# Two residual mixer layers in float32r: the operand's hi and lo parts side by side, one 512-column matmul for the hi weights

## The chip, the cores and the metric

The kernel runs on one core of one Trainium2 chip. The metric is the device time of one execution in microseconds (us). TensorE (PE) multiplies, VectorE (DVE) and ScalarE (ACT) do the elementwise work, GpSimd (POOL) does a little, SyncE (SP) issues most transfers. PEld is the weight load that goes ahead of each matmul.

## The reference

Two layers work on 256 tokens of 2048 channels. A vector c gives each layer six modulation vectors (shift, scale and gate, for the mixer and for the feed-forward):

```python
mod = cond @ w_ada[i] + b_ada[i]
h = rmsnorm(x, g_pre_mix[i]) * (1.0 + sc1) + sh1
z = h @ w_in[i]            # 2048 -> the inputs of two token mixers (GLA and RWKV-7)
...
y = jnp.concatenate([o_gla, o_rwkv], axis=-1) @ w_out[i]
x = x + gt1 * rmsnorm(y, g_post_mix[i])
h = rmsnorm(x, g_pre_ffn[i]) * (1.0 + sc2) + sh2
y = jnp.square(jax.nn.relu(h @ w_ff1[i])) @ w_ff2[i]     # 2048 -> 8192 -> 2048
x = x + gt2 * rmsnorm(y, g_post_ffn[i])
```

Everything is float32.

## The kernel before

Activations are kept channel-major: 128 channels on the partitions, 256 tokens in the free dimension, 16 such k-tiles. Each large product goes over weight tiles of 1 MB: 2048 inputs by 128 outputs. So that a fast float32r matmul keeps float32 accuracy, both sides are split into two parts. `split` (L295) rounds half of a weight tile (128x1024) to hi on ACT (L299), and takes lo = weight - hi on DVE (L300). The activations are split in the same way when they are made (hh and hl, or hid with two halves). `block_steps` (L303) then does, for each of 16 k-tiles, three matmuls of 256 columns into one half of a PSUM bank: hi weights by hi operand (L311), hi by lo (L312), lo by hi (L313). Each of them loads its own 128x128 weights. Below, one k-tile of one weight tile is called a triple.

`wtile` (L283) issues the load of a weight tile on SP's queue into one of three `wraw` buffers and splits it into four buffers of hi and four of lo, so that the split can be two weight tiles ahead. It does this at a priority that is put `AHEAD` = 100 instructions forward in the program; the scheduler of the framework orders each engine's instructions by priority when the kernel is built, and each engine then takes its queue in order. In between, `wtile` lets in modulation jobs (`ada_job`, L251): 1 MB of `w_ada` into a `wraw` buffer, and one DVE reduction of 128x2048 (L256).

The stages of a layer, in order:
- The mixers. Weight tiles of w_in are multiplied as `ORDER` says (k, q, h, g and v words), and between groups of four k-tiles (`QUANTUM`) the dependent chains of both mixers take a step: small plain float32 matmuls, ACT and DVE operations on 128x256 tiles out of a pool of 13 (`f256`). Blocks k and v leave PSUM through `lerp` (L486: ACT, then DVE); q and k of the GLA by one ACT operation each (L979, L981); gates g are read from PSUM by tanh and by DVE (L1008, L1010); the values h are a product the other way round (L993 to L995: weights are the tokens of hh and hl, moving are 256 columns of hi and lo) and leave by an ACT copy (L1000).
- w_out: 16 blocks of the mixed outputs (L1041), which leave by an ACT operation (L1042) and a square for the norm's sum.
- `boundary` (L376): residual, norm, and the first seven blocks of the next product, which grow k-tile by k-tile with `grow` (L348).
- The feed-forward, in four chunks of 16 hidden blocks: ff1 (L1061) with relu on ACT (L1068), square on DVE (L1070), split on ACT and DVE (L1072, L1073), at a priority 50 instructions ahead; then ff2 (L1077), 16 blocks that are added up over the chunks by one DVE operation a block (L1081; L1079 copies in the first chunk). Its blocks lie in six PSUM banks in turn.

The first layer's feed-forward spreads 64 modulation jobs over 118 weight tiles, the second's 16 over 100.

Of the kernel before, what the change touches and what calls it, by code (L numbers as in the profile page):

```python
# [20 lines left out]
KAPPA = 0.6065306597126334  # exp(-0.5)  # L21

# columns of the per-channel parameter table
# [65 lines left out]
GROW_LAG = 8  # pairs of k-tiles by which the first blocks' products lag behind their operand  # L89
# [7 lines left out]
def _finish(gen):  # L97
    """runs a generator to its end."""
    while True:
        try:  # L100
            next(gen)
        except StopIteration as e:
            return e.value


class Chains:
    """dependent work of several engines, in steps that are put in between the weight products."""
# [25 lines left out]
    def side_step(self):  # L133
        """one step of the chain with a pace of its own."""
# [12 lines left out]
    def run(self, blocks):  # L147
        """the blocks' steps, with the chains' steps in between."""
# [14 lines left out]
class Kernel:  # L163
    def __init__(self, tc, ctx, a):
# [4 lines left out]
        self.whi = pool("whi", 4)  # L169
        self.wlo = pool("wlo", 4)  # L170
# [9 lines left out]
    def setup(self, pool):  # L180
        nc, a, c = self.nc, self.a, self.const
        # c on four partitions
# [12 lines left out]
        # silu(c), then on all partitions  # L195
# [9 lines left out]
        # small numbers that guard roots, as bias columns  # L205
# [36 lines left out]
    def tanh(self, out, in_, bias=0.0, scale=1.0, more=()):  # L242
        """tanh, and back to the tables that the rest of the kernel uses."""
# [7 lines left out]
    def ada_job(self, i, j, single=None):  # L251
        """single: a pool for a job whose outputs are needed at once."""
# [11 lines left out]
    def ada_done(self, i, j0, j1):  # L264
        """bias, and the products with the norms' weights (and with what their roots leave out)."""
# [4 lines left out]
        # shift, scale, gate of the mixer, then of the feed-forward  # L270
# [24 lines left out]
    def split(self, half, w):  # L295
        n = half.shape[1]
        hi = self.whi.tile([P, D // 2], F32R, name="hi")[:, :n]
        lo = self.wlo.tile([P, D // 2], F32R, name="lo")[:, :n]
        self.nc.scalar.copy(hi, half)  # L299
        self.nc.vector.tensor_tensor(lo, half, hi.bitcast(F32), op=ALU.subtract)  # L300
        return hi.rearrange("p (k c) -> p k c", c=w), lo.rearrange("p (k c) -> p k c", c=w)

    def block_steps(self, src, xh, xl, order=range(KT), ps=None):  # L303
        """[128 outputs, tokens] = tile^T @ x over 16 k-tiles, in a PSUM tile."""
        nc = self.nc
        parts = self.wtile(src, P)
        if ps is None:
            ps = self.psm.tile([P, 512], F32, name="pm")[:, :T]
# [28 lines left out]
    def total(self, tiles):  # L337
        """sum over partitions (and over the tiles) on every partition."""
# [5 lines left out]
    def new_h(self):  # L344
        self.hh = self.hp.tile([P, KT, T], F32R, name="hh")
        self.hl = self.hp.tile([P, KT, T], F32R, name="hl")

    def grow(self, hi, lo, xh, xl, k, m0=0):  # L348
        """one k-tile more for the first blocks."""
# [7 lines left out]
    def first_norm(self, pool, rstd):  # L357
        """the first layer's h, k-tile by k-tile as its modulation comes in, and the first blocks of its product."""
# [6 lines left out]
        for k in range(KT):  # L365
# [8 lines left out]
            self.grow(hi, lo, self.hh[:, k], self.hl[:, k], k)  # L374
# [51 lines left out]
    def first_block(self, n, out):  # L426
        """a first block after its factor: on out, without its shift, and the shift."""
# [811 lines left out]
```

## Time and profile before

| | |
|---|---|
| median of 3 runs | 2784.63 us (2783.07 to 2787.88) |
| span of the profiled execution | 2786.0 us |
| PE / weight loads busy | 95% / 92% |
| DVE / ACT busy | 72% / 51% |
| HBM | 235 GB/s over the span |

The profile is one execution, taken by the hardware profiler. Its span runs from the first to the last instruction; the runs' times are those of executions without a profile. Matmuls are pipelined, so a record of one overlaps the next: the distance from start to start is what one costs in a stream, not its duration. "L311" is line 311 of the kernel. The names of operands are those of the program.

### The profile page before, as it was taken

The numbers are of one execution on the slowest core, as the hardware profiler recorded it, in microseconds if no ns is written. First come the engines' busy times: TensorE is split into PE (matmuls) and PEld (weight loads), VectorE is DVE, ScalarE is ACT, GpSimd is POOL, SyncE is SP. The second block draws the span as 40 slices with busy tenths as digits, with TensorE's granted clock in tenths as the row PEclk, the third lists the DMA queues.
The fourth block names the chain that finished last, engine by engine and source line by source line (L and its number), as shares of the span: only waits on it lengthen the run. The fifth ranks groups of instructions, "written<-read, shape, count | busy, mean of one in ns | idle before, by whom it ended". The sixth has DMA issues, their size and how long they took to land.

```text
span 2786.0 us, 55551 instructions
## 1 busy us (share of the span) xinstructions
PE 2658.6 (95%) x23388; PEld 2551.7 (92%) x23388; DVE 1997.1 (72%) x2961; ACT 1421.5 (51%) x2357; POOL 59.2 (2%) x153
## 2 busy tenths in 40 slices
PE   5689999999999999999999999999999999999997
PEld 4678888898999999999988889888989999999997
DVE  8997986678867777777777798655785465565655
ACT  3378644445644434434577875444474443443443
POOL 0000000000000000000001000000000000000000
PEclk8799999999999999999999999998999999999999
DMA  9775576576777777777745547654845666666653
GB/s 402 312 278 196 182 279 239 208 271 231 254 287 289 275 284 284 286 281 282 282 176 206 205 154 264 224 175 159 327 157 212 213 213 218 218 213 212 212 184 119
DMA packets 104082, 659.20 MB, mean 237 GB/s; under 512 B 11540, under 2 KB 20884, under 8 KB 32408
## 3 DMA queue, kind: packets, MB, share of 16 engines
q1 hardware_dynamic: 87848, 618.19, 61.5%
q10 hardware_dynamic: 15984, 37.46, 3.7%
q8 instruction: 183, 3.00, 0.4%
q14 instruction: 67, 0.55, 0.1%
HBM read 638.83 MB, written 16.78 MB: 235 GB/s over the span
## 4 chain that ended last, share of the span: by engine, by line
PE 84%; DVE 9%; DMA 3%; ACT 3%; issue 2%; ACTq 0%; POOL 0%; DVEq 0%; SPq 0%
PE pm L311 14%; PE pm L313 14%; PE pm L312 14%; PE px L312 8%; PE px L313 8%; PE px L311 8%; DVE raw L256 3%; DVE lo L300 2%; PE p L504 1%; DMA raw<-in_wout_dram 1%; PE pm L993 1%; PE pm L994 1%; PE px L451 1%; PE pm L995 1%; ACT hi L299 1%
## 5 line engine op out<-in xcount | busy, mean ns | idle before, releaser
L300 DVE TENSOR_TENSOR lo<-raw,hi 128x1024 fp32r<-128x1024 f32 (+1 forms) x792 | 959.7, 1216 | 544.3 <-ACT hi L299 537.8
L299 ACT CAST hi<-raw 128x1024 fp32r<-128x1024 f32 (+1 forms) x792 | 822.3, 1043 | 800.6 <-PE pm L312 356.1
L311 PE MATMUL pm<-hh,hi 128*128 128x256 f32 x2624 | 762.5, 291 | 3.6 <-ACT hi L299 1.5
L313 PE MATMUL pm<-hh,lo 128*128 128x256 f32 x2624 | 750.4, 286 | 3.9 <-DVE lo L300 3.9
L312 PE MATMUL pm<-hl,hi 128*128 128x256 f32 x2624 | 749.9, 286 | 0.0
L311 PEld LDWEIGHTS pm<-hh,hi 128*128 128x128 f32 x2624 | 504.5, 192 | 14.1 <-issue 2.0
L313 PEld LDWEIGHTS pm<-hh,lo 128*128 128x128 f32 x2624 | 504.9, 192 | 8.9 <-DVE lo L300 5.2
L312 PEld LDWEIGHTS pm<-hl,hi 128*128 128x128 f32 x2624 | 505.4, 193 | 4.6 <-issue 1.6
L256 DVE CUSTOM_DVE_ANT_0 raw<-raw,cond 128x2048 f32<-128x2048 f32 x192 | 439.0, 2287 | 38.3 <-DMA raw<-in_ada_dram 37.8
L313 PE MATMUL pm<-hid,lo 128*128 128x256 f32 x1024 | 289.0, 282 | 0.0
L313 PE MATMUL px<-hid,lo 128*128 128x256 f32 x1024 | 288.3, 282 | 0.0
L312 PE MATMUL px<-hid,hi 128*128 128x256 f32 x1024 | 288.2, 281 | 0.0
L312 PE MATMUL pm<-hid,hi 128*128 128x256 f32 x1024 | 288.0, 281 | 0.0
L311 PE MATMUL pm<-hid,hi 128*128 128x256 f32 x1024 | 287.2, 280 | 0.0
L311 PE MATMUL px<-hid,hi 128*128 128x256 f32 x1024 | 287.1, 280 | 0.0
L313 PE MATMUL px<-hh,lo 128*128 128x256 f32 x896 | 253.6, 283 | 0.0
L311 PE MATMUL px<-hh,hi 128*128 128x256 f32 x896 | 253.5, 283 | 0.0
L312 PE MATMUL px<-hl,hi 128*128 128x256 f32 x896 | 253.5, 283 | 0.0
L311 PEld LDWEIGHTS px<-hid,hi 128*128 128x128 f32 x1024 | 194.5, 190 | 0.0
L311 PEld LDWEIGHTS pm<-hid,hi 128*128 128x128 f32 x1024 | 194.4, 190 | 0.0
L313 PEld LDWEIGHTS pm<-hid,lo 128*128 128x128 f32 x1024 | 193.1, 189 | 0.0
L313 PEld LDWEIGHTS px<-hid,lo 128*128 128x128 f32 x1024 | 193.0, 189 | 0.0
(333 smaller groups left out, 4184.4 us busy)
## 6 DMA issues: line engine op xcount, KB each, us to landing
raw<-in_ff_dram SPq DMA_DIRECT2D x242, 1024.0 KB, 4.9
raw<-in_ada_dram SPq DMA_DIRECT2D x192, 1024.0 KB, 6.2
raw<-in_win_dram SPq DMA_DIRECT2D x90, 1024.0 KB, 5.1
raw<-in_wout_dram SPq DMA_DIRECT2D x32, 1024.0 KB, 5.4
raw<-in_ff1s_dram SPq DMA_DIRECT2D x16, 896.0 KB, 4.6
spill<-pk ACTq DMA_DIRECT2D x16, 640.0 KB, 4.1
pk<-spill ACTq DMA_DIRECT2D x16, 640.0 KB, 5.0
raw<-in_w_dram SPq DMA_DIRECT2D x16, 512.0 KB, 10.5
```

The costliest lines, as they stand in the source:

```text
L256: nc.vector.tensor_tensor_reduce(out=raw, in0=raw, in1=self.cond, op0=ALU.mult, op1=ALU.add, scale=1.0, scalar=0.0, accum_out=self.mod[:, ...
L299: self.nc.scalar.copy(hi, half)
L300: self.nc.vector.tensor_tensor(lo, half, hi.bitcast(F32), op=ALU.subtract)
L311: nc.tensor.matmul(ps, hi[:, n % 8], xh(k), start=n == 0, stop=False)
L312: nc.tensor.matmul(ps, hi[:, n % 8], xl(k), start=False, stop=False)
L313: nc.tensor.matmul(ps, lo[:, n % 8], xh(k), start=False, stop=n == KT - 1)
L451: self.nc.tensor.matmul(ps, self.ones, sq[:, q], start=k + q == 0, stop=k + q == KT - 1)
L504: self.nc.tensor.matmul(v[:, h, n + c], l[hs, cs], r[hs, cs], start=True, stop=True)
L993: nc.tensor.matmul(vps[c], hh[:, kk, cs], hi[:, kq], start=kk == 0, stop=False)
L994: nc.tensor.matmul(vps[c], hl[:, kk, cs], hi[:, kq], start=False, stop=False)
L995: nc.tensor.matmul(vps[c], hh[:, kk, cs], lo[:, kq], start=False, stop=kk == KT - 1)
```

## The change

The operand's hi and lo parts are put side by side in one tile ([128, 16, 2, 256]), and a PSUM bank is used in full: columns 0 to 255 take hi weights by hi operand, columns 256 to 511 take hi by lo and lo by hi. So the two matmuls with hi weights become one of 512 columns. When a block leaves PSUM its two halves are added: `halves` copies the second half to SBUF on ACT and adds the first on DVE. For the values (where hh and hl are the weights) the weights' parts hi and lo are side by side in the moving operand, and hh is loaded once for 512 columns. hi and lo of a split lie in one buffer (four of them). The square in ff1 goes from DVE to ACT. The first blocks (`grow`) keep their three matmuls.

```diff
+        hl = self.whl.tile([P, 2, D // 2], F32R, name="hl")
+        hi, lo = hl[:, 0, :n], hl[:, 1, :n]
...
+        ps = ps.rearrange("p (u t) -> p u t", u=2)
         for n, k in enumerate(order):
             hi, lo = parts[n // 8]
-            nc.tensor.matmul(ps, hi[:, n % 8], xh(k), start=n == 0, stop=False)
-            nc.tensor.matmul(ps, hi[:, n % 8], xl(k), start=False, stop=False)
-            nc.tensor.matmul(ps, lo[:, n % 8], xh(k), start=False, stop=n == KT - 1)
+            nc.tensor.matmul(ps, hi[:, n % 8], x(k), start=n == 0, stop=False)
+            nc.tensor.matmul(ps[:, 1], lo[:, n % 8], x(k)[:, 0], start=False, stop=n == KT - 1)
...
+    def halves(self, out, ps, tmp, scale=1.0):
+        nc = self.nc
+        if scale == 1.0:
+            nc.scalar.copy(tmp, ps[:, 1])
+            nc.vector.tensor_tensor(out, ps[:, 0], tmp, op=ALU.add)
+        else:
+            nc.scalar.activation(tmp, ps[:, 1], AF.Copy, scale=scale)
+            nc.vector.scalar_tensor_tensor(out, ps[:, 0], scale, tmp, ALU.mult, ALU.add)
...
     def lerp(self, i, ps, blk, out):
         nc = self.nc
+        if len(ps.shape) == 3:
+            z = self.f()
+            self.halves(z, ps, out)
+            ps = z
...
-                        nc.scalar.activation(q, ps, AF.Copy, scale=0.125)
+                        self.halves(q, ps, self.f(), 0.125)
...
-                            gps.append((yield from col(WB_GLA + 6 * n + 2 + h)))
+                            ps = yield from col(WB_GLA + 6 * n + 2 + h)
+                            gps.append(self.f())
+                            self.halves(gps[-1], ps, self.f())
...
-                nc.scalar.activation(y[:, m], ps, AF.Copy, scale=self.dcol(i, "gg1", m))
-                acc = self.accumulate(pool, acc, ps, m == KT - 1)
+                self.halves(y[:, m], ps, pool.tile([P, T], F32, name="rl"))
+                acc = self.accumulate(pool, acc, y[:, m], m == KT - 1)
+                nc.scalar.activation(y[:, m], y[:, m], AF.Copy, scale=self.dcol(i, "gg1", m))
...
-                            nc.scalar.activation(rl, ps, AF.Relu)
-                        sq = pool.tile([P, T], F32, name="sq")
-                        nc.vector.tensor_tensor(sq, rl, rl, op=ALU.mult)
+                            self.halves(rl, ps, sq)
+                            nc.scalar.activation(rl, rl, AF.Relu)
+                        nc.scalar.activation(sq, rl, AF.Square)
...
                     if c == 0:
-                        nc.scalar.copy(y[:, m], ps)
+                        nc.scalar.copy(y[:, m], ps[:, 1])
                     else:
-                        nc.vector.tensor_tensor(y[:, m], ps, y[:, m], op=ALU.add)
+                        nc.vector.tensor_tensor(y[:, m], ps[:, 1], y[:, m], op=ALU.add)
+                    nc.vector.tensor_tensor(y[:, m], ps[:, 0], y[:, m], op=ALU.add)
```

## Rows read from the trace of the kernel before

**Rows 1.** The page's part 1: busy us of each engine (share of span) and instructions.

```profile
PE 2658.6 (95%) x23388; PEld 2551.7 (92%) x23388; DVE 1997.1 (72%) x2961; ACT 1421.5 (51%) x2357; POOL 59.2 (2%) x153
```

**Rows 2.** The page's part 4: chain that ended last, by engine.

```profile
PE 84%; DVE 9%; DMA 3%; ACT 3%; issue 2%; ACTq 0%; POOL 0%; DVEq 0%; SPq 0%
```

**Rows 3.** Waits of PE: who waited for whom, us in total, times, longest.

```profile
PE pm L353 <- ACT hh L443: 42.9, 13, 8.6
...
PE pm L313 <- DVE lo L300: 3.9, 6, 1.2
```

**Rows 4.** Busy us by stretch: stretch us, PE, PEld, DVE, ACT, POOL, clock, DMA.

```profile
867.00:959.00 92.00, 92.00 (x769) 92.00 (x768) 68.97 (x83) 43.13 (x63) 0.00 (x0) 1.00 0.76 274
959.00:1050.00 91.00, 91.00 (x770) 91.00 (x770) 63.10 (x66) 34.31 (x34) 0.00 (x0) 1.00 0.79 290
...
150.00:665.00 515.00, 495.14 (x4957) 451.21 (x4956) 405.96 (x713) 289.99 (x565) 23.02 (x52) 0.99 0.68 244
1500.00:2018.00 518.00, 505.69 (x5005) 460.89 (x5005) 380.42 (x703) 295.93 (x570) 16.82 (x50) 0.98 0.60 215
...
1600.00:1700.00 100.00, 95.82 (x1326) 88.51 (x1326) 94.42 (x240) 70.92 (x124) 2.69 (x6) 1.00 0.52 181
```

**Rows 5.** Timeline of ff1, first layer: start us, us, engine, line, operation.

```profile
901.81 0.28 PE L311 MATMUL px<-hh,hi 128*128 128x256 f32 x1
901.81 0.19 PEld L312 LDWEIGHTS px<-hl,hi 128*128 128x128 f32 x1
901.93 0.28 PE L312 MATMUL px<-hl,hi 128*128 128x256 f32 x1
...
902.17 0.28 PE L311 MATMUL px<-hh,hi 128*128 128x256 f32 x1
```

**Rows 6.** Timeline of PE in the second layer's mixers: plain float32 products.

```profile
1752.09 0.81 PE L784 MATMUL px<-gl,wsmB 128*128 128x256 f32 x3
1752.73 0.38 PE L743 MATMUL px<-o,cs 128*128 128x256 f32 x1
```

**Rows 7.** Timeline of weight loads around products of 64 columns (L748).

```profile
1725.08 0.53 PEld L748 LDWEIGHTS px<-rh,at 128*128 128x128 f32 x4
...
1725.53 0.19 PEld L311 LDWEIGHTS pm<-hh,hi 128*128 128x128 f32 x1
```

**Rows 8.** Single lines: duration ns min/median/max, first and last start us.

```profile
L784 PE MATMUL px<-gl,wsmB x4: 379/379/483, 1751.8 to 1752.5; 128*128 128x256 f32 x4
...
L311 PE MATMUL px<-hh,hi x120: 283/283/283, 869.8 to 952.9; 128*128 128x256 f32 x120
...
L311 PE MATMUL pm<-hh,hi x1: 279/279/279, 180.0 to 180.0; 128*128 128x256 f32 x1
```

**Rows 9.** Timeline after that single matmul: the next weight load.

```profile
180.18 0.24 PEld L859 LDWEIGHTS p<-o 64*32 64x32 f32 x32
```

**Rows 10.** Groups from 1000 to 1300 us: busy us, mean ns | idle before, releasers.

```profile
L300 DVE TENSOR_TENSOR lo<-raw,hi 128x1024 fp32r<-128x1024 f32 x105 | 128.2, 1224 | 60.3 <-ACT hi L299 59.4 <-PE pm L313 0.9
L299 ACT CAST hi<-raw 128x1024 fp32r<-128x1024 f32 x105 | 110.0, 1052 | 132.9 <-PE pm L312 52.3 <-PE px L312 49.1 <-DMA raw<-in_ff_dram 19.0
L256 DVE CUSTOM_DVE_ANT_0 raw<-raw,cond 128x2048 f32<-128x2048 f32 x28 | 64.1, 2289 | 10.9 <-DMA raw<-in_ada_dram 10.9
...
L1070 DVE TENSOR_TENSOR sq<-rl 128x256 f32<-128x256 f32 x27 | 11.3, 420 | 0.0
L1072 ACT CAST hid<-sq 128x256 fp32r<-128x256 f32 x27 | 11.0, 408 | 40.5 <-DVE sq L1070 40.5
...
L1068 ACT ACTIVATE rl<-px 128x256 f32<-128x256 f32 x14 | 5.3, 376 | 0.0
```

**Rows 11.** Waits of ACT: who waited for whom, us in total, times, longest.

```profile
ACT hi L299 <- PE pm L312: 356.1, 242, 3.7
...
ACT hid L1072 <- DVE sq L1070: 154.5, 114, 3.7
...
ACT hi L299 <- DMA raw<-in_wout_dram: 52.0, 17, 5.9
```

More of the change, by code (lines that the diff above doesn't have):

```diff
@@ L168, in __init__ @@
         self.wraw = pool("wraw", 3)
-        self.whi = pool("whi", 4)
-        self.wlo = pool("wlo", 4)
+        self.whl = pool("whl", 4)
         self.hp = pool("hp", 1)
@@ L296, in split, with block_steps @@
         n = half.shape[1]
-        hi = self.whi.tile([P, D // 2], F32R, name="hi")[:, :n]
-        lo = self.wlo.tile([P, D // 2], F32R, name="lo")[:, :n]
+        hl = self.whl.tile([P, 2, D // 2], F32R, name="hl")
+        hi, lo = hl[:, 0, :n], hl[:, 1, :n]
         self.nc.scalar.copy(hi, half)
         self.nc.vector.tensor_tensor(lo, half, hi.bitcast(F32), op=ALU.subtract)
+        if w > P:
+            return hl.rearrange("p u (k c) -> p u k c", c=w)
         return hi.rearrange("p (k c) -> p k c", c=w), lo.rearrange("p (k c) -> p k c", c=w)
-    def block_steps(self, src, xh, xl, order=range(KT), ps=None):
+    def block_steps(self, src, x, order=range(KT), ps=None):
         nc = self.nc
@@ L344, in new_h @@
     def new_h(self):
-        self.hh = self.hp.tile([P, KT, T], F32R, name="hh")
-        self.hl = self.hp.tile([P, KT, T], F32R, name="hl")
+        self.h = self.hp.tile([P, KT, 2, T], F32R, name="h")
     def grow(self, hi, lo, xh, xl, k, m0=0):
@@ L900, in mixers @@
         nc, a = self.nc, self.a
-        hh, hl = self.hh, self.hl
+        hx = self.h
         def col(b):
@@ L909, in col @@
                 return z
-            return (yield from self.block_steps(a["win"][i, b], lambda k: hh[:, k], lambda k: hl[:, k]))
+            return (yield from self.block_steps(a["win"][i, b], lambda k: hx[:, k]))
         self.spread([(0, j) for j in range(32, 80)] if i == 0 else [(1, j) for j in range(ADA_FF0, 80)], 58)
@@ L978, in blocks @@
                         ps = yield from col(b0)
-                        nc.scalar.activation(q, ps, AF.Copy, scale=0.125)
+                        self.halves(q, ps, self.f(), 0.125)
                         ps = yield from col(b0 + 1)
-                        nc.scalar.copy(k, ps)
+                        self.halves(k, ps, self.f())
                         chains.post(word, (f"h{n - 2}",) if n >= 2 else (), self.gla_scores(i, n, q, k))
@@ L985, in blocks @@
                         n = int(n)
-                        vps = [self.psm.tile([P, 512], F32, name="pm")[:, :T] for _ in range(2)]
+                        vps = [self.psm.tile([P, 512], F32, name="pm").rearrange("p (u t) -> p u t", u=2)
+                               for _ in range(2)]
                         for half in range(2):
-                            for quarter, (hi, lo) in enumerate(self.wtile(a["win"][i, WB_GLA + 6 * n + 4 + half], 256)):
+                            for quarter, hl in enumerate(self.wtile(a["win"][i, WB_GLA + 6 * n + 4 + half], 256)):
                                 for c in range(2):
@@ L992, in blocks @@
                                         kk = half * 8 + quarter * 4 + kq
-                                        nc.tensor.matmul(vps[c], hh[:, kk, cs], hi[:, kq], start=kk == 0, stop=False)
-                                        nc.tensor.matmul(vps[c], hl[:, kk, cs], hi[:, kq], start=False, stop=False)
-                                        nc.tensor.matmul(vps[c], hh[:, kk, cs], lo[:, kq], start=False,
+                                        nc.tensor.matmul(vps[c], hx[:, kk, 0, cs], hl[:, :, kq], start=kk == 0,
+                                                         stop=False)
+                                        nc.tensor.matmul(vps[c][:, 1], hx[:, kk, 1, cs], hl[:, 0, kq], start=False,
                                                          stop=kk == KT - 1)
@@ L999, in blocks @@
                         for c in range(2):
-                            nc.scalar.copy(vt[:, c], vps[c])
+                            self.halves(vt[:, c], vps[c], self.f())
                         chains.post(word, (f"q{n}",), self.gla_mix(i, n, vt))
@@ L1028, in layer @@
                 self.mixers(i)
-                oh = self.hp.tile([P, KT, T], F32R, name="hh")
-                ol = self.hp.tile([P, KT, T], F32R, name="hl")
+                ox = self.hp.tile([P, KT, 2, T], F32R, name="h")
                 for k in OUT_ORDER:
-                    nc.scalar.copy(oh[:, k], self.o[:, k])
-                    nc.vector.tensor_tensor(ol[:, k], self.o[:, k], oh[:, k].bitcast(F32), op=ALU.subtract)
+                    nc.scalar.copy(ox[:, k, 0], self.o[:, k])
+                    nc.vector.tensor_tensor(ox[:, k, 1], self.o[:, k], ox[:, k, 0].bitcast(F32), op=ALU.subtract)
             fp = ctx.enter_context(self.tc.tile_pool(name=f"fp{i}", bufs=1))
@@ L1040, in layer @@
             for m in range(KT):
-                ps = self.block(a["wout"][i, m], lambda k: oh[:, k], lambda k: ol[:, k], OUT_ORDER)
-                nc.scalar.activation(y[:, m], ps, AF.Copy, scale=self.dcol(i, "gg1", m))
-                acc = self.accumulate(pool, acc, ps, m == KT - 1)
+                ps = self.block(a["wout"][i, m], lambda k: ox[:, k], OUT_ORDER)
+                self.halves(y[:, m], ps, pool.tile([P, T], F32, name="rl"))
+                acc = self.accumulate(pool, acc, y[:, m], m == KT - 1)
+                nc.scalar.activation(y[:, m], y[:, m], AF.Copy, scale=self.dcol(i, "gg1", m))
             jobs = [(i, j) for j in range(80, 96)] + [(1, j) for j in range(ADA_FF0) if i == 0]
@@ L1053, in bank @@
                 nb += 1
-                return self.psm.tile([P, 512], F32, name="pm")[:, :T] if nb % 2 else self.bank()[:, :T]
+                return self.psm.tile([P, 512], F32, name="pm") if nb % 2 else self.bank()
             for c in range(4):
@@ L1060, in layer @@
                     if not first:
-                        ps = self.block(a["ff1"][i, c * 16 + n], lambda k: hh[:, k], lambda k: hl[:, k], ps=bank())
+                        ps = self.block(a["ff1"][i, c * 16 + n], lambda k: hx[:, k], ps=bank())
                     with self.tc.high_priority(FF_AHEAD):
                         rl = pool.tile([P, T], F32, name="rl")
+                        sq = pool.tile([P, T], F32, name="sq")
                         if first:
@@ L1076, in layer @@
                 for m in range(KT):
-                    ps = self.block(a["ff2"][i, c * 16 + m], lambda k: hid[k][:, 0], lambda k: hid[k][:, 1], ps=bank())
+                    ps = self.block(a["ff2"][i, c * 16 + m], lambda k: hid[k], ps=bank())
                     if c == 0:
-                        nc.scalar.copy(y[:, m], ps)
+                        nc.scalar.copy(y[:, m], ps[:, 1])
                     else:
-                        nc.vector.tensor_tensor(y[:, m], ps, y[:, m], op=ALU.add)
+                        nc.vector.tensor_tensor(y[:, m], ps[:, 1], y[:, m], op=ALU.add)
+                    nc.vector.tensor_tensor(y[:, m], ps[:, 0], y[:, m], op=ALU.add)
                     if c == 3:
```

8 lines of the change are left out of this document (4 added, 4 removed).

## The prediction, made before the result was known

> **What bounds the kernel now.** I read the page's part 1 first [rows 1]: TensorE (PE) is busy 95% of the span, its weight loads 92%, VectorE (DVE) 72%, ScalarE (ACT) 51%. A busy PE need not be the bound, so the chain that ended last comes next [rows 2]: PE carries 84% of it. Then the waits of PE [rows 3]: the longest (42.9 us) lies in the first layer's start, which the change doesn't touch; for the split of the weights, PE waited 3.9 us in all. So in the weight products PE waits for next to nobody, and the time is the number of matmuls by their spacing. The windows show it: in a chunk of ff1, 768 matmuls fill 92 us without a gap, in one of ff2 91 us [rows 4]. The single records [rows 5] give the spacing: 901.81 to 902.17 us is 0.36 us for three, 120 ns each (ff2: 91/768 = 118.5 ns). Each matmul has its own weight load beside it.
>
> **What is replaced.** A "triple" is one k-tile of one weight tile: hi by xh, hi by xl, lo by xh, 360 ns now (ff2 355.5). Afterwards it is one 512-column and one 256-column matmul, the same 768 columns with two weight loads instead of three. The triples: ff1 has 57 blocks a layer outside the first ones, 114 x 16 = 1824; ff2 128 x 16 = 2048; w_out 32 x 16 = 512; the mixers 74 blocks x 16 + 8 value tiles x 32 = 1440. Sum 5824.
>
> **What a 512-column matmul costs** isn't in the trace for this operand, so I bound it. 256 columns at 2.4 GHz are 106.7 ns, and 120 are spent: what the other 13 ns are decides the case.
> - Low end, 214 ns: the plain float32 matmuls of the chains (L784) take twice as long a column; three of them go from 1752.09 to 1752.73 us, 0.64/3 = 213 ns for 256 columns [rows 6], which is 512 array cycles with a weight load under them and nothing on top. A load by itself is shorter: L748's products have 64 columns, and four loads go from 1725.08 to 1725.53, 112 ns each [rows 7]. So 120 ns could be a load of 112 ns, somewhat slowed, with the matmul waiting for it; under 512 columns it would hide.
> - High end, 240 ns: the 120 ns are 0.47 ns a column whatever the loads do, and 512 columns cost twice as much.
> - Between them: durations. L784's lasts 379 ns, of which 213 are streaming, so 166 are the way through the array; ff1's lasts 283, and one that had no load under it 279 [rows 8] (the next load, of L859, began 0.2 us later [rows 9]). So an overlapped load lengthens a matmul by 4 ns, and without one it streams for 279 - 166 = 113 ns, 6 more than its columns. If these 6 are per column, 512 columns take 213 + 12 + 4 = 229; if they are only length of the way, 214. I take the middle, 221.
>
> The 256-column matmul behind it keeps its 120 ns (118.5 in ff2), since the next load can only start when it starts: in [rows 5] each load starts with the matmul before its own. A triple is then 221 + 120 = 341, 19 less; in ff2 221 + 118.5 = 339.5, 16 less. Gross: ff1 1824 x 19 = 34.7; ff2 2048 x 16 = 32.8; w_out 512 x 19 = 9.7; mixers 1440 x 19 = 27.4; sum 104.6 us.
>
> On this the Trainium skill speaks ("TensorE: Matmul & The Clock Gate", section "Part 2: What happens when you issue a matmul"): weight loads have a read port of their own and take no bandwidth from the matmul that runs. The 283 against 279 ns [rows 8] speak against it by 4 ns. By the rule the 512 columns would sit at the low end.
>
> **What is added, and where it lands.** Costs per operation are in [rows 10]: split on ACT 1.05 us, on DVE 1.22, a modulation job on DVE 2.29, a 256-column DVE operation 0.42, an ACT eviction 0.38, an ACT cast 0.41.
> - ff1: the eviction is now ACT copy, DVE add, ACT relu, ACT square, ACT cast, DVE subtract (before: relu, DVE square, cast, subtract). ACT gains 0.38 + 0.41 a block, DVE none. With 16 x 341 = 5.46 us a block ACT has 2 x 1.05 + 0.38 + 3 x 0.41 = 3.7 us of work, but in order: second split 1.05, copy 0.38, wait for DVE (its split 1.22 and the add 0.42, of which the copy hides 0.38: some 1.4), three operations 1.2, first split 1.05: 5.1 us. That just fits. With a modulation job in front of the add (2.29) it is 7.4. In the first layer 64 jobs lie over 118 tiles, 0.54 a block; if each hits the wrong place, 5.1 + 0.54 x 2.29 = 6.3, over the 5.76 of now; if none does, 5.1. What hides this now: ACT already waits 154.5 us for DVE's square, and far more for PE to free its buffers [rows 11], which is slack; the split runs up to two blocks ahead. I let the first layer's ff1 lose half of its gain, 57 x 16 x 19 / 2 = 8.7 us. The second layer has 0.16 jobs a block and keeps it.
> - ff2: one more DVE add a block, 0.42 us. DVE is busy 63.1 of 91 us there [rows 4]; 16 blocks add 6.7, so 70 of 87. Hidden.
> - w_out: ACT and DVE get 0.4 us a block, hidden; but ACT waited 52 us for w_out's own DMA [rows 11], in 17 waits of up to 5.9 us, as the three raw buffers are shared with modulation jobs. A faster PE meets this transfer. I keep a third of the gain and lose 6.5.
> - Mixers: 90 evictions (42 lerp, 16 q and k, 16 gates, 16 value halves) get a DVE add of 0.42, some an ACT copy, and more f256 buffers out of 13. DVE is busy 406 of 515 us in the first layer's mixers and w_out, 380 of 518 in the second's, and 94.4 of 100 in 1600 to 1700 [rows 4]. About 19 us more a layer on an engine at 79% and 73% is no bound on average, but is in stretches like that one. I keep half: 13.7 lost.
> - Ends of stages: the last block's eviction is longer by one DVE add (ff2, 0.42) or by copy and add (w_out, about 0.8), twice each: 2.5; the first MM of w_out needs both halves of its operand, 0.4 twice. 3 us.
>
> SP's queue, the transfers and their sizes are as before; buffers for the split parts are merged in pairs, the same bytes. Priorities are counted in instructions, and a block has 32 matmuls rather than 48, so leads of 50, 100 or 150 reach half as far again; two blocks of split buffers limit it, so I cost it at nothing, and at some us in the mixers if it delays the inverse.
>
> **Sum.** 104.6 - 8.7 - 6.5 - 13.7 - 3 = 72.7 us off the profiled execution's span of 2786.0, 2713.3. The three timed runs have a median of 2784.6, 1.4 less: 2712.
>
> **Rivals.**
> 1. The load hides wholly (low end): a triple is 214 + 120 = 334, 26 less (23 in ff2): 1824 x 26 + 2048 x 23 + 512 x 26 + 1440 x 26 = 145 us, less the same shares (11.9 + 8.9 + 18.7 + 3 = 42.5): 102, 2682. For it: L784. Against it: 279 against 166 + 107.
> 2. The cost is per column (high end, 240): no gain, and the longer evictions stay, 3 to 15 us: 2788 to 2800, say 2792. For it: 113 of the 120 ns are there without a load. Against it: the four ns with a load, and that ff2's same columns take 118.5. [...]
> 3. The other side, slower: evictions in the mixers put themselves between the splits and the chains. DVE's add waits for ACT's copy, and behind it stand the splits and the chains' steps that PE takes in order. If each of 90 costs PE one split's time, 1.2 us, that is 108 us against a gain outside the mixers of 34.7 - 8.7 + 32.8 + 3.2 - 3 = 59: 49 slower, 2834. It decides from 59/90 = 0.66 us each. Against it: the cover is two blocks, 11 us, and PE's waits for the split are 3.9 us now [rows 3].
> 4. Half of this again is lost: ff1's ACT and DVE cycle lands at 6.3 us in the first layer, and w_out and the mixers give nothing: 17.4 + 32.8 - 57 x (6.3 - 5.76) - 3 = 16 gain, 2768.
>
> **How the numbers follow.** Forecast 2712 (its own range 2695 to 2745): 0.45. Rival 1: 0.20. Rival 2: 0.13. Rival 3: 0.07. Rival 4: 0.15. A measurement of this kernel tells about 0.2%, 5.6 us, from no change. Faster: 0.45 + 0.20 + 0.14 of rival 4 = 0.79. Same: 0.04 of rival 2 and 0.01 of rival 4 = 0.05. Slower: 0.09 + 0.07 = 0.16. The range leaves out rivals 2 and 3 (0.20) and reaches to rival 1 with fewer losses and to rival 4: 2655 to 2772.
>
> **What would show it.** The spacing in ff1 after the change: 341 ns from one 512-column start to the next (334 rival 1, 360 rival 2). A chunk of ff2 lasting 87 us instead of 91. ff1 of the first layer at 5.5 to 5.7 us a block while the second's is at 5.46; where ACT's wait for DVE's add grows to several hundred us, rival 4. PE waits for the split well over 3.9 us, or gaps at L504 and L859 in the mixers, would be rival 3. The forecast is wrong first of all if the 512-column matmul isn't within 214 to 229 ns.

## The result: slower, and the profile after

The changed kernel takes 2818.2 us (median of 4 runs, 2814.5 to 2825.5) against 2786.3 (2783.1 to 2787.9) before: 1.0124 times as long, 95% interval 1.0104 to 1.0144. That is 32 us slower where 73 us faster were forecast. The profiled execution's span is 2812.8 us.

The page's part 1 (busy us, share of the span, instructions), the head of part 4 and three groups of part 5 (busy us, mean ns of one, idle time before and its releaser) of the changed kernel:

```profile
PE 2623.7 (93%) x17564; PEld 2243.1 (80%) x17564; DVE 2078.7 (74%) x3197; ACT 1540.1 (55%) x2687; POOL 65.2 (2%) x153
...
PE 79%; DVE 6%; ACT 4%; DMA 4%; issue 2%; ACTq 0%; DVEq 0%
...
L314 PE MATMUL pm<-h,hl 128*128 128x512 f32 x2624 | 960.9, 406 | 18.9 <-DVE y L325 11.7
L315 PE MATMUL pm<-h,hl 128*128 128x256 f32 x2624 | 748.6, 286 | 3.7 <-DVE hl L299 3.7
...
L1088 ACT ACTIVATE rl<-rl 128x256 f32<-128x256 f32 x114 | 47.4, 416 | 111.8 <-DVE rl L325 111.4
```

Against [rows 1] PE has 5824 instructions fewer and is busy for 35 us less, yet its share fell from 95 to 93% and its part of the chain from 84% [rows 2] to 79%: what PE gained it now waits away. It is idle for 189 us of the span instead of 127, 62 more. Its waits (line waited, releaser, us in total, times, longest):

```profile
PE pm L364 <- ACT h L454: 44.1, 13, 8.8
PE p L874 <- DVE f L838: 16.6, 6, 4.2
...
PE pm L314 <- DVE y L325: 11.7, 2, 7.4
PE px L533 <- DMA wsmA<-in_wsm_dram: 11.4, 5, 3.6
PE p L874 <- DVE sc L876: 8.3, 8, 3.0
PE px L893 <- DVE vt L325: 8.1, 3, 4.2
PE p L519 <- DVE pk L589: 6.5, 2, 3.4
...
PE pm L315 <- DVE hl L299: 3.7, 2, 2.9
```

The first line is the start, as in [rows 3], and the wait for the split (last line) is 3.7 us, 3.9 before; with the other lines that wait for a split it is 7.5, and was 7.0. Grown are the waits of the chains' scores (L874, L519; before 6.0 us of the first kind, shown further below), and new are those for DVE's add of an eviction (L325), by L314 and by the product that uses the values (L893).

By stage, each limited by the last records of its kind in the trace (last product of the first blocks, last split of the mixed operand, sums of a norm's squares); us, sums over both layers, in profiled executions:

| kernel | mixers | w_out | feed-forward | span |
|---|---|---|---|---|
| before | 447.4 + 461.3 | 88.5 + 87.1 | 694.9 + 694.6 | 2786.0 |
| after | 469.1 + 480.1 | 90.5 + 93.9 | 686.8 + 680.0 | 2812.8 |

The mixers lost 40.5, w_out 8.8, the feed-forward gained 22.7; starts and boundaries stayed within 1 us.

**The gain itself is small.** Start us, us, line of PE in the first layer's ff1, and below it ff2:

```profile
900.57 0.40 PE L314 MATMUL px<-h,hl 128*128 128x512 f32 x1
900.81 0.28 PE L315 MATMUL px<-h,hl 128*128 128x256 f32 x1
900.93 0.40 PE L314 MATMUL px<-h,hl 128*128 128x512 f32 x1
...
903.05 0.40 PE L314 MATMUL px<-h,hl 128*128 128x512 f32 x1
...
989.72 0.39 PE L314 MATMUL pm<-hid,hl 128*128 128x512 f32 x1
...
991.47 0.40 PE L314 MATMUL px<-hid,hl 128*128 128x512 f32 x1
```

From 900.57 to 903.05 lie seven triples, 354 ns each, and from 989.72 to 991.47 five, 350 ns: 6 less than the 360 and 355.5 of before, where 19 and 16 were forecast.

**The loss is waiting, not work.** Busy us by stretch (stretch us, PE, PEld, DVE, ACT, POOL, clock, DMA) of the changed kernel, both layers' mixers and then two stretches of the second's:

```profile
131.00:600.00 469.00, 427.25 (x3658) 344.37 (x3658) 371.53 (x715) 279.18 (x569) 30.21 (x51) 0.95 0.59 213
1487.00:1967.00 480.00, 441.05 (x3733) 357.40 (x3733) 350.15 (x716) 288.87 (x591) 21.30 (x50) 0.95 0.52 184
...
1620.00:1640.00 20.00, 20.00 (x129) 16.68 (x128) 19.05 (x46) 14.32 (x28) 0.00 (x0) 1.00 0.79 286
1640.00:1660.00 20.00, 12.28 (x257) 9.73 (x255) 16.68 (x51) 12.52 (x26) 1.11 (x2) 0.74 0.30 111
```

In the mixers PE idles 80.7 us of 949, where before it idled 35.6 of 908 (the rows of before stand beside those of f19 below), and DVE's share is 79 and 73%, as before. So DVE isn't fuller; PE waits for single results. In the 20 us in which it waited 7.7, the granted clock fell from 1.00 to 0.74, between the levels of 2.4 and 1.2 GHz. What it waited for (PE, then DVE and ACT):

```profile
1642.80 0.45 PE L874 MATMUL p<-f 64*32 64x32 f32 x32 [0.91 <-DVE sc L876]
1646.53 0.47 PE L874 MATMUL p<-f 64*32 64x32 f32 x32 [3.29 <-DVE f L838]
...
1644.07 1.95 DVE L633 STREAM_TRANSPOSE o<-o 128x1024 f32<-128x1024 f32 x1 [0.42 <-ACT o L632]
1646.10 0.28 DVE L838 TENSOR_TENSOR f<-f,o 128x128 f32<-128x128 f32 x1
...
1641.94 2.09 ACT L632 COPY o<-at 32x1024 f32<-32x1024 f32 x2
1644.06 0.42 ACT L832 ACTIVATE f<-f 128x256 f32<-128x256 f32 x1
```

The GLA's score chain (L832, L838, L874) needs an ACT and a DVE operation of 0.3 to 0.4 us each, and finds the blockwise inverse's copy (2.09 us) and transpose (1.95 us) in front of them. No eviction stands in front in this place: what decides is the order in which the queue was built, not how full an engine is.

### The profile page after: what moved, and what is told of

The parts are those of the page before. It is cut to its first block, busy times and chain, and to the rows that moved or that the text cites. A ratio compares the mean times of both kernels' runs of the same rounds, so it can differ in the third digit from the quotient of the medians.

```text
span 2812.8 us, 44108 instructions
## 1 busy us (share of the span) xinstructions
PE 2623.7 (93%) x17564; PEld 2243.1 (80%) x17564; DVE 2078.7 (74%) x3197; ACT 1540.1 (55%) x2687; POOL 65.2 (2%) x153
## 4 chain that ended last, share of the span: by engine, by line
PE 79%; DVE 6%; ACT 4%; DMA 4%; issue 2%; ACTq 0%; DVEq 0%
PE pm L314 27%; PE px L314 15%; PE pm L315 14%; PE px L315 7%; DVE hl L299 2%; PE pm L1009 2%; ACT hl L298 2%; PE p L519 1%; DMA raw<-in_ff_dram 1%; PE px L462 1%; PE pm L1011 1%; DMA raw<-in_ada_dram 1%; DMA wsmA<-in_wsm_dram 1%; DVE raw L255 1%; PE px L783 1%
## 5 line engine op out<-in xcount | busy, mean ns | idle before, releaser
L299 DVE TENSOR_TENSOR hl<-raw,hl 128x1024 fp32r<-128x1024 f32 (+1 forms) x792 | 959.2, 1216 | 494.0 <-ACT hl L298 491.5
L298 ACT CAST hl<-raw 128x1024 fp32r<-128x1024 f32 (+1 forms) x792 | 821.1, 1041 | 682.9 <-PE pm L315 320.2
L314 PE MATMUL pm<-h,hl 128*128 128x512 f32 x2624 | 960.9, 406 | 18.9 <-DVE y L325 11.7
L315 PE MATMUL pm<-h,hl 128*128 128x256 f32 x2624 | 748.6, 286 | 3.7 <-DVE hl L299 3.7
L314 PEld LDWEIGHTS pm<-h,hl 128*128 128x128 f32 x2624 | 497.8, 190 | 141.4 <-issue 18.2
L315 PEld LDWEIGHTS pm<-h,hl 128*128 128x128 f32 x2624 | 500.3, 191 | 10.9 <-DVE hl L299 4.3
L314 PE MATMUL px<-hid,hl 128*128 128x512 f32 x1024 | 362.3, 395 | 2.8 <-DVE hid L1092 2.8
L314 PE MATMUL pm<-hid,hl 128*128 128x512 f32 x1024 | 362.8, 395 | 0.0
L314 PE MATMUL px<-h,hl 128*128 128x512 f32 x896 | 316.7, 396 | 0.0
L314 PEld LDWEIGHTS px<-hid,hl 128*128 128x128 f32 x1024 | 193.5, 189 | 49.6 <-DVE hid L1092 4.7
L314 PEld LDWEIGHTS pm<-hid,hl 128*128 128x128 f32 x1024 | 194.3, 190 | 45.2
L314 PEld LDWEIGHTS px<-h,hl 128*128 128x128 f32 x896 | 168.2, 188 | 40.6
L315 PEld LDWEIGHTS pm<-hid,hl 128*128 128x128 f32 x1024 | 193.4, 189 | 0.3
L315 PEld LDWEIGHTS px<-hid,hl 128*128 128x128 f32 x1024 | 192.7, 188 | 0.0
L315 PEld LDWEIGHTS px<-h,hl 128*128 128x128 f32 x896 | 168.8, 188 | 0.3 <-DVE hl L299 0.3
```

What stands on the lines that cost most here:

```text
L314: nc.tensor.matmul(ps, hi[:, n % 8], x(k), start=n == 0, stop=False)
L315: nc.tensor.matmul(ps[:, 1], lo[:, n % 8], x(k)[:, 0], start=False, stop=n == KT - 1)
```

## The experiments

The changed kernel's parts were first taken apart: two theories, T1 that the evictions cost, T2 that the matmuls with their leads do. Times stand beside those of the kernel before on the same chip; where no interval is given a time is one execution. Only the main edit of a run is printed; "..." marks what is left out.

**Evictions alone (e1_evict).** Three matmuls again, the same in the values' products; all else as changed:

```diff
-nc.tensor.matmul(ps, hi[:, n % 8], x(k), ...)
+nc.tensor.matmul(ps[:, 0], hi[:, n % 8], x(k)[:, 0], ...)
+nc.tensor.matmul(ps[:, 1], hi[:, n % 8], x(k)[:, 1], ...)
```

> The evictions alone: the three 256-column matmuls of before, written to the two halves of a bank, and every block leaves PSUM as in the changed kernel, by ACT copy and DVE add. Theory T1 (the longer way out of PSUM is what costs the mixers): the mixers' stages stay at some 475 and 485 us (447 and 461 before, 469 and 480 changed, which has some 6 us of faster matmuls each), the feed-forwards go back to 695, the whole to 2830 to 2840. Theory T2 (the leads, counted in instructions, reach half as far again because a block has 32 matmuls instead of 48): the mixers go back to 447 and 461, the whole to 2785 to 2795.

2838.7 against 2789.3: 49 slower, mixers 471.2 + 482.7.

**Matmuls alone (e2_mm).** The 512- and 256-column matmuls, with the evictions of before on the first half; the products in the second half are computed and left out of the output:

```diff
-self.halves(q, ps, self.f(), 0.125)
+nc.scalar.activation(q, ps[:, 0], AF.Copy, scale=0.125)
...
```

> The matmuls alone: the 512-column matmul and the one of 256 columns as changed, but every block leaves PSUM as before, from the first half of its bank; the products with the lo parts are computed and left out of the output. T1: the mixers come to 440 and 455 us, the feed-forwards to 675 to 680, the whole to about 2740. T2: the mixers stay at 465 to 480, the whole at 2795 to 2805.

2744.3, 45 faster; mixers 434.9 + 461.7, feed-forward 682.2 + 680.8. T1 holds: the matmuls bring 45 and the evictions cost more than that. But 45 is less than half of the forecast's gross 104.6. The run keeps the merged buffers and the long leads of the change, so it isn't the price of the matmuls alone.

**The change in the feed-forward alone (e3_ffonly).** Mixers and w_out have three matmuls and the old evictions; weights and operand stay side by side:

```diff
-ps = self.block(a["wout"][i, m], lambda k: ox[:, k], OUT_ORDER)
+ps = _finish(self.block3_steps(a["wout"][i, m], lambda k: ox[:, k], OUT_ORDER))
...
```

> The change in the feed-forward alone: mixers and w_out have the three matmuls and the evictions of before, on the merged tiles. Both T1 and T2 leave the mixers at 447 and 461 us and the feed-forwards at 687 and 680, so the whole at 2763 (0.992 of before). If the merged operand and weight tiles themselves cost the mixers something, they stay above 455 and 470.

2780.3, ratio 0.9974 [0.9954, 0.9994]. The feed-forward kept its gain (687.2 + 680.0), but the first layer's mixers and w_out, with no work changed, took 22.7 us more than before, and the second's 3.3 less. Taken up below.

**Shorter leads (e4_leads, and f16_leads3: the same kernel in several rounds).** A block now has 32 matmuls, so the leads are cut to two thirds:

```diff
-AHEAD = 100
-AHEAD_STEP = 50
-FF_AHEAD = 50
-LATE = (150, 60)
+AHEAD = 67
+AHEAD_STEP = 33
+FF_AHEAD = 33
+LATE = (100, 40)
```

> The changed kernel with the leads put back to the same number of blocks: 67 instead of 100, 33 instead of 50, and the inverse put back by 100 and 40 instead of 150 and 60. T2: the mixers come to about 441 and 455 us, the whole to 2770 to 2780. T1: no change, 2805 to 2820.

> The changed kernel with leads that reach as far as before in blocks (67, 33, 33, inverse put back by 100 and 40), once more and in several rounds, as its single execution (2785.7) can't be told from before. If the 32 us against the changed kernel (2818) are the leads, the median lies at 2780 to 2792 and the ratio to before is within 0.997 to 1.003. If that execution was a lucky one, the median lies above 2800.

2785.7, and in 10 runs 2791.3 against 2789.3, ratio 1.0005 [0.9994, 1.0016]. So four constants are worth 30 us (32 slower became 2 slower). Neither theory had it: T1 expected nothing, T2 more. One place, the second layer's w_out, holds 12 of the 21.5 us between the two profiled executions and shows how. DVE's and ACT's timeline in the changed kernel, at its start, and PE's one long wait there:

```profile
1968.67 1.23 DVE L299 TENSOR_TENSOR hl<-raw,hl 128x1024 fp32r<-128x1024 f32 x1 [0.50 <-ACT hl L298]
1978.74 2.29 DVE L255 CUSTOM_DVE_ANT_0 raw<-raw,cond 128x2048 f32<-128x2048 f32 x1 [8.84 <-DMA raw<-in_ada_dram]
...
1983.23 0.42 DVE L325 TENSOR_TENSOR y<-pm,rl 128x256 f32<-128x256 f32 x1
...
1971.72 0.36 ACT L324 COPY rl<-pm 128x256 f32<-128x256 f32 x1
...
PE pm L314 <- DVE y L325: 7.4, 1, 7.4
```

ACT had copied the half at 1971.7, but DVE's add came at 1983.2: a modulation job stood ahead of it and waited 8.8 us for its transfer, and PE 7.4 us for the bank. With the short leads (f16) a job in the same place waited 1.6 us, and w_out took 81.8 us instead of 93.9:

```profile
1960.18 2.29 DVE L255 CUSTOM_DVE_ANT_0 raw<-raw,cond 128x2048 f32<-128x2048 f32 x1 [1.62 <-DMA raw<-in_ada_dram]
```

Before, DVE also waited 4.7 us for such a job in that place, but there ACT alone frees the bank. The chains' waits fall with the leads too (f16; in the changed kernel these two are 16.6 and 6.5 us):

```profile
PE p L874 <- DVE f L838: 8.3, 4, 3.4
...
PE p L519 <- DVE pk L589: 4.3, 1, 4.3
```

**What the columns cost (m1_cols).** A kernel of its own: series of 128 matmuls, each with a weight load, the width stepped up:

```diff
+for n in range(128):
+    nc.tensor.matmul(ps[:, :320], w[:, n % 16], f512(n % 16)[:, :320], ...)
```

> A kernel of its own that leaves the two layers out and times the matmul alone: eleven series of 128 float32r matmuls, each with its own 128x128 weight load, of 256, 320, 384, 448 and 512 columns, 512 with the two halves 258 apart, 512 and 256 in turn, 256 with one weight tile or one operand tile throughout, and 256 and 512 with 64 weight columns. If the 120 ns of 256 columns are a cost per column: 120, 150, 180, 210, 240 ns. If they are columns and a fixed price of some 13 ns for each matmul or load: 120, 147, 173, 200, 227. If the load is the bound at 256 columns and hides from there on: 120, 136, 163, 189, 216. With 64 weight columns a price of the load halves: 113 and 220; a price per column stays.

Its timeline (start us, us of the series, line), and below the last rows of the alternation and the series with 64 weight columns:

```profile
27.64 15.52 PE L1165 MATMUL pm<-h,w 128*128 128x256 f32 x128
42.99 18.94 PE L1169 MATMUL pm<-h,w 128*128 128x320 f32 x128
61.76 22.35 PE L1173 MATMUL pm<-h,w 128*128 128x384 f32 x128
83.95 26.61 PE L1177 MATMUL pm<-h,w 128*128 128x448 f32 x128
110.40 29.22 PE L1181 MATMUL pm<-h,w 128*128 128x512 f32 x128
139.46 29.92 PE L1185 MATMUL pm<-hid,w 128*128 128x512 f32 x128
169.22 0.40 PE L1189 MATMUL pm<-h,w 128*128 128x512 f32 x1
...
213.59 15.51 PE L1194 MATMUL pm<-h,w 128*128 128x256 f32 x128
...
244.30 14.68 PE L1202 MATMUL pm<-h,w 128*64 128x256 f32 x128
258.81 29.60 PE L1206 MATMUL pm<-h,w 128*64 128x512 f32 x128
```

The distance of two starts over 128 is one matmul: 256 columns 119.9 ns, 320 146.6, 384 173.4, 448 206.6, 512 227.0. From 256 to 512 that is 107.1 ns for 256 columns, 0.418 ns each, which is 2.4 GHz (448 lies 6 ns above this line), and 119.9 less 256 of these leaves 13 ns that each matmul pays whatever its length. With half of the weight columns 256 cost 113.4 (from 244.30 to 258.81), 6.5 less, half of the 13 ns. At 512 columns half of the weight columns saves nothing (230 ns by the first and last start of that series), so whether the 13 ns belong to the load or to each matmul stays open. Either way they aren't hidden under longer streaming, which was expected to give 216 for 512 columns: a triple of two matmuls instead of three saves one price of 13 ns, which the alternation shows: (213.59 - 169.22) / 128 = 346.6 ns. The kernel's own 350 and 354 lie above. An operand whose halves stand apart (L1185) costs 232.5 instead of 227.0; ff2's operand lies so, which may be part of its 350, but the halves of ff1's, at 354, are adjacent.

**Which words, buffers, engine.** On the shorter leads, so against 2785.7 and 2791.3 (before, on the chip of these three: 2791.0 in one execution; mixers 462.3 + 474.6 and 460.4 + 481.2; so one stage of one kernel differs by up to 6.6 us between executions, and smaller differences say nothing). e5_kvnew gives the q, h and g words their old matmuls and evictions back, e6_qhgnew the k and v words; e7_fbufs has 15 buffers of 128x256 instead of 13:

```diff
 # e5_kvnew (e6_qhgnew: the two exchanged)
-yield from self.block_steps(a["win"][i, b], ...)
+yield from (self.block3_steps if b >= WB_GLA else self.block_steps)(a["win"][i, b], ...)
...
 # e7_fbufs
-F_BUFS = 13
+F_BUFS = 15
```

> On e4_leads: in the mixers the words q, h and g have the three matmuls and the evictions of before (by ACT alone), the words k and v keep the 512-column matmul and their eviction by copy, add and lerp. Theory T1a (what costs is that q, k, values and gates of the GLA now pass DVE's queue before their chain can start): the mixers come from 462 and 475 to 445 to 450 and 455 to 460 us. T1b (all evictions cost alike, by DVE's work): 10 of 44 and 10 of 46 go in the k words and 32 in v, so more than half of the loss stays, 455 and 470. T1c (the f256 buffers): gates and q, k take most of the added ones, so also 445 to 450.

> On e4_leads, the other half: q, h and g as changed, k and v with the three matmuls and the eviction of before. T1a: the mixers stay at 462 and 475 or go above by the matmuls that are slower again, 465 and 478. T1b: 452 and 465.

> e4_leads with 15 f256 buffers instead of 13. T1c: the mixers come down by most of the loss, to 450 and 462 us. T1a and T1b: no change, 462 and 475 within 4 us.

2783.7 (mixers 450.7 + 477.3), 2786.6 (461.8 + 473.5) and 2784.7 (460.5 + 475.0). Only e5's first layer, 10 us, stands out of the spread: q, h and g cost more there than their matmuls bring. The second layer doesn't follow, so which words cost is left open; buffers aren't it. Then the way out itself (both runs leave the products in the second half out of the output):

```diff
 # e10_act, in the mixers
 nc.scalar.copy(tmp, ps[:, 1])
-nc.vector.tensor_tensor(out, ps[:, 0], tmp, op=ALU.add)
+nc.scalar.copy(out, ps[:, 0])
 # e11_dve, in the mixers
-nc.scalar.copy(tmp, ps[:, 1])
-nc.vector.tensor_tensor(out, ps[:, 0], tmp, op=ALU.add)
+nc.vector.tensor_scalar(out, ps[:, 0], scale, None, ALU.mult)
```

> On e4_leads, with the evictions of the mixers by two ACT copies and without DVE's add (the second half is copied and left out of the output). If what costs the mixers is DVE, by its time or its queue: they come from 462 and 475 to 440 to 450 and 455 to 462 us. If it is ACT's added copy or the mere length of the way out: they stay at 460 to 470 and 473 to 480.

> The other half of that: the evictions of the mixers by one DVE operation on the first half of the bank, no ACT copy ahead of it (the second half is left out of the output). If DVE is the cause: the mixers stay at 458 to 465 and 470 to 477 us. If ACT's copy or the length is: 440 to 450 and 455 to 462.

2793.8 and 2778.9 against 2785.1 before: sparing DVE gains nothing, one operation fewer gains 7 to 12, mostly in the first layer. So it isn't DVE's load; the length of the way fits, but by a difference not far above the spread.

**Evictions without merged buffers, merged buffers without evictions, long leads alone.** e3's 22.7 us had two possible sources left: hi and lo in one buffer, or an order that came out otherwise by itself. Merging, evictions and reach were each done alone: f14 and f15 edit the kernel before, f19 takes e1 and f17 the kernel with shorter leads, both with two pools again (f17 so with three matmuls in the values' products):

```diff
 # f14_merged
-        hi = self.whi.tile([P, D // 2], F32R, name="hi")[:, :n]
-        lo = self.wlo.tile([P, D // 2], F32R, name="lo")[:, :n]
+        hl = self.whl.tile([P, 2, D // 2], F32R, name="hl")
+        hi, lo = hl[:, 0, :n], hl[:, 1, :n]
 # f15_longer
-AHEAD = 100
-AHEAD_STEP = 50
-FF_AHEAD = 50
-LATE = (150, 60)
+AHEAD = 150
+AHEAD_STEP = 75
+FF_AHEAD = 75
+LATE = (225, 90)
 # f19_evsep and f17_sep
-        hl = self.whl.tile([P, 2, D // 2], F32R, name="hl")
-        hi, lo = hl[:, 0, :n], hl[:, 1, :n]
+        hi = self.whi.tile([P, D // 2], F32R, name="hi")[:, :n]
+        lo = self.wlo.tile([P, D // 2], F32R, name="lo")[:, :n]
```

> The kernel before with one edit: hi and lo of a split lie in one buffer (four of them) instead of two pools of four. Every matmul and eviction is that of before. In the kernel with the change in the feed-forward alone, the mixers and w_out with their old work on merged tiles took 461.7 + 96.9 us in the first layer against 447.4 + 88.5 before, and 456.8 + 88.3 against 461.3 + 87.1 in the second: 19 us in all. Theory M (the merged buffers themselves cost, as ACT's next split waits for the last lo matmul as well): 10 to 20 us slower than before, most of it in mixers and w_out. Theory N (they cost nothing; the 19 us are the spread between single executions and an order that came out otherwise): within 6 us of before.

> The kernel before with its leads half again as long, in the old count of 48 matmuls a block: AHEAD 150, its step 75, the feed-forward's 75, the inverse put back by 225 and 90. That is how far the leads reach in the kernel with the change, with nothing else of it. The changed kernel gained 32 us in one execution from leads cut by a third. Theory L (the reach by itself costs, whatever the matmuls are): before becomes 15 to 30 us slower, in the mixers first. Theory E (the reach costs only together with the longer evictions): within 6 us of before, at most 10 slower.

> The evictions of the change alone, with everything else of before: three matmuls of 256 columns into the two halves, hi and lo in two pools, leads as before. The kernel with evictions and merged buffers took 2838.7, the one with merged buffers alone 2815.3, before 2789.3. If the costs add up: 2789 + 23 = 2812, 2803 to 2821. If the evictions cost only where merged buffers have already made the splits late: 2785 to 2798.

> The changed kernel with leads cut by a third (as before, 2791 in several rounds) and with hi and lo of a split again in two pools of four buffers; so that they needn't be side by side, the values' products take three matmuls of 256 columns into the two halves again (256 triples that give up 7 to 14 ns each, 2 to 4 us). If merging the buffers cost 26 us in the changed kernel too, as it did in the old one alone: 2791 - 26 + 3 = 2768, 2760 to 2776. If merging costs only in the old order of work: 2788 to 2798.

- f14: 2815.3 against 2789.3, ratio 1.0096 [1.0075, 1.0117]. An edit that adds no instruction and no byte costs 26 us in the old kernel.
- f15: 2797.9, ratio 1.0032 [1.0014, 1.0049]: the long reach alone costs 9, not 30.
- f19: 2838.6 against 2785.2, ratio 1.018 [1.0149, 1.0211]: the evictions alone cost 53 us without merged buffers, about as much as with them (e1).
- f17: 2792.0 against 2785.2, ratio 1.0024 [1.0006, 1.0042]: in the changed kernel, separate buffers give nothing back.

So my sum of single costs fell: merging costs 26 beside the old evictions and nothing beside the new. Both change the order that the scheduler builds, and a merged buffer also comes free only with its lo matmul; the runs don't separate the two. f14 shows the same picture as above, in its first w_out:

```profile
597.45 2.29 DVE L255 CUSTOM_DVE_ANT_0 raw<-raw,cond 128x2048 f32<-128x2048 f32 x1 [7.36 <-DMA raw<-in_ada_dram]
599.67 2.36 DVE L299 TENSOR_TENSOR hl<-raw,hl 128x1024 fp32r<-128x1024 f32 x2
...
PE pm L312 <- DVE hl L299: 5.8, 4, 4.2
```

A modulation job was put in front of two splits and waited 7.4 us, and PE 4.2 behind it. The w_out took 95.4 us instead of 88.5. That is 7 of the 24 us between the profiled executions; 17 lie in the mixers, where no such place was singled out. For f19 the busy times of the two layers' mixers (stretch us, PE, PEld, DVE, ACT, POOL, clock, DMA) are read, first of before, then of f19, then of f14:

```profile
132.00:579.00 447.00, 425.35 (x4362) 380.67 (x4361) 353.26 (x669) 266.66 (x536) 22.30 (x50) 0.98 0.64 226
1473.00:1934.00 461.00, 447.02 (x4496) 401.46 (x4495) 335.16 (x669) 282.95 (x563) 21.04 (x51) 0.97 0.55 191
```

```profile
131.00:605.00 474.00, 433.44 (x4359) 388.28 (x4359) 368.62 (x714) 279.48 (x567) 22.66 (x50) 0.95 0.60 213
1503.00:1984.00 481.00, 448.06 (x4498) 403.76 (x4496) 349.00 (x716) 291.60 (x591) 20.65 (x50) 0.96 0.53 183
```

```profile
132.00:588.00 456.00, 432.47 (x4384) 387.60 (x4383) 354.06 (x670) 270.03 (x540) 20.14 (x51) 0.98 0.62 219
1489.00:1958.00 469.00, 449.03 (x4500) 403.75 (x4500) 335.79 (x670) 282.48 (x569) 21.32 (x51) 0.97 0.54 189
```

With the same matmuls f19's mixers are 47 us longer. PE idles 73.5 us instead of 35.6, 38 more, and is busy for 9 more, at a clock of 0.95 and 0.96 instead of 0.98 and 0.97. (That the clock makes these 9 isn't shown: f14's mixers are busy for 9 more too, at the clock of before.) DVE has 29 us more work, but in the longer time a share of 78 and 73%, against 79 and 73%: it is no fuller. 47 us over 90 evictions are 0.52 each.

**A version that beats both.** e13_best has mixers and w_out as before, two pools, the change in the feed-forward alone, and there leads cut by a third; f18_wout has the change in w_out as well:

```diff
 # e13_best, against the kernel before, in the feed-forward alone
-FF_AHEAD = 50
+FF_AHEAD = 33
...
-self.ahead = min(AHEAD, self.ahead + AHEAD_STEP)
+self.ahead = min(self.lead, self.ahead + AHEAD_STEP)
...
+            self.lead = 67
             for c in range(4):
                 hid = []
 # f18_wout, against e13_best
...
-ps = _finish(self.block3_steps(a["wout"][i, m], lambda k: ox[:, k], OUT_ORDER))
+ps = self.block(a["wout"][i, m], lambda k: ox[:, k], OUT_ORDER)
```

> A version for the result: mixers and w_out as before, with hi and lo parts of the weights in two pools as before, the 512-column matmul in the feed-forwards alone, and there the leads put back to the same number of blocks (67 and 33). From the stages: 447 + 89 + 681 + 461 + 87 + 679 and what is unchanged, 2757 (0.990 of before). If the merged weight tile was not what took e3_ffonly's first mixers to 462 and w_out to 97, they stay there and the whole comes to 2775.

> The best kernel so far (mixers and w_out with the old work, hi and lo in two pools, one 512-column matmul in the feed-forward alone, its leads cut by a third: 2768.6) with the change in w_out as well: 512 triples at 7 to 14 ns less, 4 to 7 us, against evictions longer by a copy and an add off PE's path, and the ends of two stages later by 0.8 us each. Theory: 2760 to 2766, 2 to 5 us off. If w_out's own transfers take it back (ACT waited 52 us for them before): 2768.

2768.6 against 2785.1, ratio 0.9928 [0.99, 0.9957], and 2763.4 against 2785.2, ratio 0.9917 [0.9891, 0.9943]; their intervals overlap, so w_out's gain isn't shown. f18's stages: mixers 448.0 + 456.9, w_out 91.1 + 87.3, feed-forward 687.4 + 679.6.

## Why the prediction was wrong

It missed by 105 us, 73 faster to 32 slower, in three steps; the rival that came true is the third.

1. **The price of 512 columns (gross gain 104.6, measured 45).** The step that failed is the choice of 221 between 214 and 229. Two readings misled it. The low end took three plain float32 matmuls at 213 ns [rows 6] as 512 cycles with the load hidden; the float32r matmul pays 13 ns at 256 columns and at 512 alike, so that row doesn't carry over to it. And the durations (283 against 279 [rows 8]) put only 4 of the 13 ns down to the load and left 6 open between the columns and the way through the array, where m1's series gives 13 at either length: a duration isn't spacing, and one matmul without a load is too few. The series' 227.0 lies within the range that was to decide, 214 to 229; in the kernel the 512 cost 230 to 240, outside it, and the 256 behind it 115 to 120, where "keeps its 120 ns" was right. A triple lands between the forecast's 341 and rival 2's 360; the feed-forward gained 26.5 in e2 where 3872 triples at 19 and 16 gave 67.5 before losses. At the series' 346.6 a triple the gross gain would be 69, so the mis-sized price explains 36 of the 59.6 that are missing; the other 24, between the series and the kernel, are open. On the Trainium skill's rule from the prediction ("TensorE: Matmul & The Clock Gate", section "Part 2: What happens when you issue a matmul": loads take no read bandwidth from the running matmul), m1 is divided: at 256 columns 64 weight columns fewer save 6.5 ns, which speaks against it, at 512 they save nothing (230 against 227.0).
2. **Leads, "I cost it at nothing" (measured 30).** The cover named, two blocks of split buffers, limits how far the splits run ahead, but not where modulation jobs and chain steps land in DVE's and ACT's queues. f15 prices the reach at 9 beside old evictions; with the new ones the bank too hangs on DVE's queue, and it costs 30.
3. **Evictions in the mixers (losses of 31.9 in all, measured 53, of which 47 in the mixers).** I halved the mixers' gain because DVE, at 79 and 73% on average, is full only in stretches. Rival 3 had the mechanism: the chains' steps, which PE takes in order. Its deciding price of 0.66 us counted on a gain of 59 outside the mixers; with 0.52 each against 22.7 in the feed-forward it decided all the same. The sign the prediction named for it, gaps at L504 and L859, is what came: L519 and L874 in the new numbering, with 31 us of waits (16.6 + 8.3 + 6.5), where the kernel before had these:

```profile
PE p L859 <- DVE f L823: 6.0, 5, 2.4
...
PE p L859 <- issue: 3.2, 3, 1.5
```

   Half of the 31 belongs to step 2: with the evictions and shorter leads the three sum to 15 us (8.3 + 4.3 + 2.6 in f16). Rival 3's other half, late splits, didn't come: 3.7 us.

The sum: 59.6 missing, 21.5 more lost, 30 not counted, 111 against 105; the rest of 6 isn't settled (e2 is one execution). It is a tally and not a proof: e2 has the merged buffers and the long leads in it, and these costs didn't add up elsewhere. Right were the feed-forward's eviction (ACT waits 111 us for the add, not the several hundred of rival 4, and the first layer's ff is 6.8 us above the second's where 8.7 were forecast; with shorter leads, 682.7 in f16, within 2), the boundaries, and the start.

Not settled: why a triple costs 350 and 354 in the kernel against 346.6 in the series, which words of the mixers cost, and how much of the 53 us is the longer way and how much an order that could be put right by hand. That merging alone moves 26 us says that the second can be large.

## What to carry to other kernels

Where chains of small operations on three engines are woven between large products, an operation added to each way out is priced by who stands in line behind it, not by its 0.4 us: measure it by putting in the evictions alone, with the old matmuls. When the number of instructions changes, every distance that is counted in instructions changes with it; rescale these first. And take the price of a new matmul shape from the slope of several lengths, not from durations or from another data type, and expect the kernel to lie above it (here by 3 to 8 ns a triple, unexplained).

## What was unexpected of the hardware

- A float32r matmul with its own 128 weight columns costs its columns at 2.4 GHz and 13 ns more, at 256 as at 512 columns (119.9 and 227.0); 64 weight columns take 6.5 off at 256. At 512 columns they took none: (288.0 - 258.8) / 127 = 230 ns by the series' first and last start, which I can't explain.
- The same 512 columns cost 227.0 or 232.5 ns with the operand's halves adjacent or with their starts 258 columns apart, a gap of two.
- Where PE waited 7.7 of 20 us, the granted clock of that stretch was 0.74, between the levels of 1.2 and 2.4 GHz; in the 20 us ahead of it, without a gap, it was 1.00.
